# Spreading the matmul blocks of a feed-forward layer over PSUM banks

## The chip, the cores and the metric

The kernel runs on one core of one Trainium2 chip. A core has a matrix engine (TensorE, "PE" in the profile, with its weight loads listed as "PEld"), a vector engine (DVE), a scalar engine (ACT), a general engine (POOL) and a queue that issues DMAs (SP). The metric is the device time of one launch in microseconds.

Matmuls write into PSUM. The kernel uses it in tiles of 128 partitions by 512 float32 columns; one such tile is one bank, and there are eight. A matmul here is 128 by 128 weights against 256 moving columns, so its output fills half a bank.

## The reference

The reference is a two-layer encoder trunk on 256 tokens of width 1024. Each layer is a feed-forward half-step, a token mixer (retention, stick-breaking attention, a state-space mixer, and an output projection), and a second feed-forward half-step. All of them are normalised and modulated by a vector `c`. What the change touches is the feed-forward:

```
def swiglu(u, wg, wu, wd):
    return (jax.nn.silu(u @ wg) * (u @ wu)) @ wd

h = h + 0.5 * (1.0 + mod[:, :, 2]) * swiglu(u, ffn1_wg[l], ffn1_wu[l], ffn1_wd[l])
```

The inner width is 2816, which is eleven groups of 256. There are four feed-forward half-steps in all, two in each layer.

## The kernel before

Everything is kept transposed: partitions are features, columns are the 256 tokens. To keep float32 accuracy, each operand is split into a rounded part and a remainder (`hi` and `lo` of a weight, `uh` and `ul` of an activation), and each product is three matmuls onto the same output (`mm3`, L208): hi by uh, hi by ul, lo by uh. These three are the "block of three matmuls" of the change.

**Weights.** 184 units of weights of 1 MB each come from HBM by DMA in a fixed order, into tiles called `raw`, mixed with 80 units `raw_a` of the modulation matrices. `step` (L271) takes the next one. For half a weight unit, ACT makes `hi` (L322) and DVE makes `lo` (L323); for a modulation unit, DVE reduces it against the condition (L282). `half(n, f)` (L317) first emits the splits up to seven halves ahead (`AHEAD = 7`) of the half that is wanted. There are eight buffers each for `hi` and `lo`.

**Feed-forward** (`ffn`, L583). For each group `j` of 256 inner columns there are a gate weight `g`, an up weight `u` and a down weight `d`. `proj` (L567) accumulates gate over eight feature blocks `k`: for each `k`, one block of three into columns 0 to 255 of the bank `pg`, and one into columns 256 to 511, 48 matmuls in all. ACT then applies silu to the whole bank `pg` into an SBUF tile `sg` (L627, through L203). `proj` does the same for up in another bank, `pu`. DVE multiplies `sg` by `pu` (L630), and ACT and DVE split the product into the tile `g`. Where `j` is 1, gate and up are interleaved by `k` (`proj2`) before silu. The first two weight units of a half-step (in the first half-step, the first six) are done earlier, into banks `ld`, while the normalisation is still under way.

**Down.** `out_unit` (L517) takes one group: for each half `f` of it and each of eight output blocks `d`, one block of three into an accumulator `dn`. Four banks hold the eight accumulators, two to a bank, side by side (L519). It is called for earlier groups, so that the product `g` has time to be made. The last `out_unit` goes by output block, and DVE adds each finished block to the residual `h` (L539) while the later blocks are computed. The mixer's output projection uses `out_unit` too, with accumulators `wo`.

**Mixer.** Its input projections `pj` also put both blocks of a `k` into one bank. The two value projections (`pv`) have a bank for each of two token halves, and there the activations are the stationary operand and the weights move. `conv` reads a bank `pj` by halves: ACT makes the first term of each half (L715), DVE adds the others (L717). At the start of three of the half-steps `ends` fills the SBUF tile `sg` by halves in the same way (ACT through L203, DVE at L601).

**Banks.** Four banks are a ring (`bank`, L213) from which `pg` and `pu` come in turn, so that a bank comes round every second group; four are the accumulators. [...]

**Order.** Each engine runs its own instructions in the order in which the program emits them (a manual schedule). The framework puts the semaphore waits between engines in by itself, from which tiles the instructions read and write.

Of the kernel before, what the change touches and what calls it, by code (L numbers as in the profile page):

```python
# [10 lines left out]
ALU = mybir.AluOpType  # L11
PSUM = bass.MemoryType.PSUM

P = 128
# [68 lines left out]
def downs(j, g0):  # L83
    done = 0
    for i in range(g0, j + 1):
        lo = done
        done = i if i - lo <= 2 else lo + 2
    return range(lo, done)
# [74 lines left out]
class Trunk:  # L163
# [352 lines left out]

    def out_unit(self, accs, n, mov, first, last, gate):  # L517
        nc = self.nc
        dst = lambda d: accs[d // 2][:, (d % 2) * 256:(d % 2) * 256 + 256]  # L519

        def block(w, d, f):
            st = first and f == 0 and d % 2 == 0
            self.mm3(dst(d), [w[0][:, d * P:(d + 1) * P], w[1][:, d * P:(d + 1) * P]], mov[f], st)

        if not last:
            for f in range(2):
                w = self.half(n, f)
                for d in range(8):
                    block(w, d, f)
                    if d % 2:  # L530
                        self.tick()
            return
        ws = [self.half(n, 0, 7), self.half(n, 1, 6)]
        for b in range(4):
            for d in (2 * b, 2 * b + 1):
                for f in range(2):
                    block(ws[f], d, f)
            for d in (2 * b, 2 * b + 1):
                nc.vector.scalar_tensor_tensor(out=self.h[:, d], in0=dst(d), scalar=gate[:, d:d + 1], in1=self.h[:, d],  # L539
                                               op0=ALU.mult, op1=ALU.add)  # L540
            if self.hg is None and b == 2:
                nc.scalar.preload_act_table_set(SET_SQRT)
            self.norm_a(b)
            if b == 2 or self.hg and b:
                self.norm_b(b - 1)
        if self.hg:
            self.norm_b(3)
# [10 lines left out]
    def proj_k(self, bank, w, k, flip, banks):  # L558
        w = [t[:, k % 4] for t in w]
        for f in range(2):  # L560
            if flip:
                self.mm3(banks[f], w, [t[:, f * P:(f + 1) * P] for t in self.u(k)], k == 0, True)
            else:
                cs = slice(f * P, (f + 1) * P)
                self.mm3(bank[:, f * 256:(f + 1) * 256], [t[:, cs] for t in w], self.u(k), k == 0 and f == 0)
# [17 lines left out]
    def ffn(self, w0, gate_col, prep, start=None):  # L583
        nc = self.nc
        self.open_acc(False)
        n = w0 + 2
        pend = []

        def gated(sg):
            g = self.tk4("g", FR)  # L590
            gh, gl = (g[:, 2 * i:2 * i + 2] for i in range(2))
            flat = lambda t: t.rearrange("p a b -> p (a b)")
            self.split(flat(gh), flat(gl), sg)
            pend.append([(gh[:, f], gl[:, f]) for f in range(2)])

        def ends(f, t, b):
            v = sg[:, (f % 2) * 256:(f % 2) * 256 + 256]
            if f < 2:
                self.silu(out=v, in_=t, bias=b)
            else:  # L600
                nc.vector.scalar_tensor_tensor(out=v, in0=t, scalar=b, in1=v, op0=ALU.add, op1=ALU.mult)  # L601

        g0 = 1
        if start:
            g0 = GS
            banks = start()
            n = w0 + 2 * GS
            self.need(n, 0, 2)
            for j in range(GS):
                sg = self.tk2("sg")  # L610
                self.silu(out=sg, in_=banks[2 * j])
                nc.vector.tensor_tensor(out=sg, in0=sg, in1=banks[2 * j + 1], op=ALU.mult)
                gated(sg)
        else:
            sg = self.tk2("sg")
            self.lead(w0, ends)
            gated(sg)
        accs = None
        for j in range(g0, NJ):
            pg, pu = self.bank("pg"), self.bank("pu")  # L620
            pair = j == 1
            if pair:
                self.proj2(n, (pg, False, None), (pu, False, None))
            else:
                self.proj(pg, n)
            sg = self.tk2("sg")
            self.silu(out=sg, in_=pg)  # L627
            if not pair:
                self.proj(pu, n + 1)
            nc.vector.tensor_tensor(out=sg, in0=sg, in1=pu, op=ALU.mult)  # L630
            gated(sg)
            if j == g0:
                accs = [self.acc("dn") for _ in range(4)]
            n += 2
            for i in downs(j, g0):
                self.out_unit(accs, n, pend.pop(0), i == 0, False, None)
                n += 1
            if start and j == 7:
                nc.sync.dma_start(out=self.consts, in_=self.io["consts"])
                nc.sync.dma_start(out=self.wdt, in_=self.io["wdt"])  # L640
        gate = self.gate(gate_col, True)
        prep()
        self.out_unit(accs, n, pend.pop(0), False, True, gate)
        self.close_acc()
# [469 lines left out]
```

## Time and profile before

| | |
|---|---|
| three runs | 1124.79, 1131.02, 1131.15 us; median 1131.02 |
| the profiled execution | 1130.79 us, its span 1129.0 us |
| PE busy | 1094.3 us, 97% of the span, 9316 matmuls |
| DVE busy | 892.1 us, 79% |
| ACT busy | 617.4 us, 55% |
| DMA | 282.63 MB, 250 GB/s on the mean |
| mean granted TensorE clock | 0.998 |

The profile is one execution, and 1.8 us of its time lie outside the span. A row of a group view gives the source line, the engine, the output and inputs by tile name, the shapes, the count, the busy time and the mean duration of one, and then the idle time of the engine just before these instructions with what ended it. A row of the timeline gives start, length, and in brackets how long the engine had been idle and what released it. Consecutive instructions of a kind are merged there, with their count. A row of the chain of work that ended last gives start, length, engine, tile and count. A matmul's own duration overlaps the next matmul's, so the pace of PE is read from starts, or from the length of a stretch over its count.

The half-steps lie, by matmuls of gate, up and down, at 63 to 210 us (the first), 400 to 569 us, 582 to 757 us and 948 to 1116 us; the two mixers fill most of what is between.

### The profile page before, as it was taken

The page shows a single profiled execution, that of the slowest core. Times are in us where ns is not written, and L with a number is a line of the kernel's source. Part 1 is how long each engine was busy: PE and PEld are TensorE (multiplying, and loading weights), DVE is VectorE, ACT ScalarE, POOL GpSimd, SP SyncE. Part 2 cuts the span into 40 slices and gives each one's busy share as a digit, 9 for nine tenths or more (in the row PEclk, how much of TensorE's full clock was granted, in tenths as well). Part 3 has the DMA queues.
Part 4 walks back from the last instruction along what each step waited for, and adds up shares of the span by engine and source line. Part 5 has one row for each costly group of instructions (what it writes and reads, how often), then busy time and mean ns, then how long its engine had stood idle before and what let it go on. Part 6 is the DMA issues. An engine that isn't in the chain of part 4 may idle for free.

```text
span 1129.0 us, 22045 instructions
## 1 busy us (share of the span) xinstructions
PE 1094.3 (97%) x9316; PEld 1083.1 (96%) x9316; DVE 892.1 (79%) x1300; ACT 617.4 (55%) x870; POOL 0.2 (0%) x4
## 2 busy tenths in 40 slices
PE   1999999999999999999999999999999999999996
PEld 0999999999999999999999999999999999999996
DVE  6989896888778788899688888667886878987644
ACT  3463535586874464445466444457687546554442
POOL 0000000000000000000000000000000000000000
PEclk9999999999999999999999999999999999999999
DMA  9979998467454449999627888653745552898611
GB/s 374 352 262 375 364 372 332 148 222 273 177 187 150 187 145 375 355 369 365 236 97 298 337 328 320 250 185 125 285 179 196 187 187 75 337 342 325 234 69 38
DMA packets 39555, 282.63 MB, mean 250 GB/s; under 512 B 4384, under 2 KB 4640, under 8 KB 5408
## 3 DMA queue, kind: packets, MB, share of 16 engines
q1 hardware_dynamic: 39456, 281.22, 66.1%
q8 instruction: 73, 1.20, 0.4%
q14 instruction: 26, 0.21, 0.1%
HBM read 280.15 MB, written 1.05 MB: 249 GB/s over the span
## 4 chain that ended last, share of the span: by engine, by line
PE 96%; DVE 2%; ACT 1%; DMA 1%; issue 0%; SPq 0%; ACTq 0%; DVEq 0%
PE dn L206 21%; PE pg L206 18%; PE pu L206 18%; PE pj L206 14%; PE ld L206 8%; PE wo L206 6%; PE pv L206 4%; DVE raw_a L282 1%; PE seg L206 1%; PE nps L206 1%; PE tail L206 1%; PE sz L206 1%; DMA h<-in_x 1%; PE rn L206 1%; PE yb L206 1%; PE rs L206 0%
## 5 line engine op out<-in xcount | busy, mean ns | idle before, releaser
L323 DVE TENSOR_TENSOR lo<-raw_w,hi 128x1024 fp32r<-128x1024 f32 x368 | 440.9, 1222 | 126.6 <-ACT hi L322 126.0
L322 ACT ACTIVATE hi<-raw_w 128x1024 fp32r<-128x1024 f32 x368 | 379.5, 1054 | 239.8 <-DMA raw_w<-in_w 122.5
L206 PE MATMUL dn<-g,hi 128*128 128x256 f32 x1408 | 243.6, 277 | 0.0
L206 PEld LDWEIGHTS dn<-g,hi 128*128 128x128 f32 x1408 | 212.9, 188 | 0.0
L282 DVE CUSTOM_DVE_ANT_0 raw_a<-raw_a,cond,params 128x1024 f32<-128x1024 f32 x160 | 198.9, 1280 | 0.0
L206 PE MATMUL dn<-g,lo 128*128 128x256 f32 x704 | 195.2, 277 | 0.0
L206 PE MATMUL pg<-ul,hi 128*128 128x256 f32 x608 | 168.6, 277 | 0.0
L206 PE MATMUL pg<-uh,hi 128*128 128x256 f32 x608 | 168.6, 277 | 0.0
L206 PE MATMUL pg<-uh,lo 128*128 128x256 f32 x608 | 168.5, 277 | 0.0
L206 PE MATMUL pu<-uh,hi 128*128 128x256 f32 x608 | 168.5, 277 | 0.0
L206 PE MATMUL pu<-ul,hi 128*128 128x256 f32 x608 | 168.5, 277 | 0.0
L206 PE MATMUL pu<-uh,lo 128*128 128x256 f32 x608 | 168.5, 277 | 0.0
L206 PEld LDWEIGHTS dn<-g,lo 128*128 128x128 f32 x704 | 132.9, 189 | 0.0
L206 PE MATMUL pj<-uh,hi 128*128 128x256 f32 x448 | 126.4, 282 | 0.0
L206 PE MATMUL pj<-ul,hi 128*128 128x256 f32 x448 | 124.5, 278 | 0.0
L206 PE MATMUL pj<-uh,lo 128*128 128x256 f32 x448 | 124.5, 278 | 0.0
L206 PEld LDWEIGHTS pu<-uh,lo 128*128 128x128 f32 x608 | 114.8, 189 | 0.0
L206 PEld LDWEIGHTS pg<-uh,lo 128*128 128x128 f32 x608 | 114.7, 189 | 0.0
L206 PEld LDWEIGHTS pg<-uh,hi 128*128 128x128 f32 x608 | 114.1, 188 | 0.0
L206 PEld LDWEIGHTS pg<-ul,hi 128*128 128x128 f32 x608 | 114.1, 188 | 0.0
L206 PEld LDWEIGHTS pu<-uh,hi 128*128 128x128 f32 x608 | 114.1, 188 | 0.0
L206 PEld LDWEIGHTS pu<-ul,hi 128*128 128x128 f32 x608 | 114.1, 188 | 0.0
(189 smaller groups left out, 1788.7 us busy)
## 6 DMA issues: line engine op xcount, KB each, us to landing
raw_w<-in_w SPq DMA_DIRECT2D x184, 1024.0 KB, 5.5
raw_a<-in_ada SPq DMA_DIRECT2D x80, 1024.0 KB, 6.4
consts<-in_consts SPq DMA_DIRECT2D x1, 1216.0 KB, 9.6
h<-in_x SPq DMA_DIRECT2D x1, 1024.0 KB, 6.7
out<-fin SPq DMA_DIRECT2D x4, 256.0 KB, 2.3
cond<-in_c SPq DMA_DIRECT2D x1, 512.0 KB, 4.5
mats<-in_mats SPq DMA_DIRECT2D x1, 256.0 KB, 6.9
params<-in_params SPq DMA_DIRECT2D x1, 176.0 KB, 4.7
```

Source lines behind the costliest of these rows:

```text
L206: self.nc.tensor.matmul(out, lhsT=lhsT, rhs=rhs, start=start, stop=True, skip_group_check=True)
L282: nc.vector.tensor_tensor_reduce(out=raw[:, f * 1024:(f + 1) * 1024], in0=raw[:, f * 1024:(f + 1) * 1024], in1=self.cond, scale=1.0, scala ...
L322: self.nc.scalar.activation(out=hi, in_=src, func=AF.Copy)
L323: self.nc.vector.tensor_tensor(out=lo, in0=src, in1=hi.bitcast(F32), op=ALU.subtract)
```

## The change

Gate and up of a group no longer have a bank each. The group takes two banks from the ring (now tagged by the name `pgu`); gate uses columns 0 to 255 of both, up uses columns 256 to 511 of both. So the two blocks of three of one `k` go to different banks. silu and the multiplication become two instructions of 256 columns each, one per bank. In `out_unit`, accumulator `d` goes to bank `d % 4`, half `d // 4`, where it was bank `d // 2`, half `d % 2`, so consecutive blocks go round the four banks. The `start` flags follow: gate sets them at `k` 0 on both banks, up on none, and down on blocks 0 to 3. `proj` and `proj_k` get `flip=None` for the new layout, with the last argument used as the flag for `start`.

```
     def out_unit(self, accs, n, mov, first, last, gate):
-        dst = lambda d: accs[d // 2][:, (d % 2) * 256:(d % 2) * 256 + 256]
+        dst = lambda d: accs[d % 4][:, (d // 4) * 256:(d // 4) * 256 + 256]
 
         def block(w, d, f):
-            st = first and f == 0 and d % 2 == 0
+            st = first and f == 0 and d < 4
...
             if flip:
                 self.mm3(banks[f], w, [t[:, f * P:(f + 1) * P] for t in self.u(k)], k == 0, True)
+            elif flip is None:
+                cs = slice(f * P, (f + 1) * P)
+                self.mm3(bank[f], [t[:, cs] for t in w], self.u(k), k == 0 and banks)
...
         for j in range(g0, NJ):
-            pg, pu = self.bank("pg"), self.bank("pu")
+            two = [self.bank("pgu") for _ in range(2)]
+            pg, pu = ([t[:, o:o + 256] for t in two] for o in (0, 256))
             pair = j == 1
             if pair:
-                self.proj2(n, (pg, False, None), (pu, False, None))
+                self.proj2(n, (pg, None, True), (pu, None, False))
             else:
-                self.proj(pg, n)
+                self.proj(pg, n, None, True)
             sg = self.tk2("sg")
-            self.silu(out=sg, in_=pg)
+            for f in range(2):
+                self.silu(out=sg[:, f * 256:(f + 1) * 256], in_=pg[f])
             if not pair:
-                self.proj(pu, n + 1)
-            nc.vector.tensor_tensor(out=sg, in0=sg, in1=pu, op=ALU.mult)
+                self.proj(pu, n + 1, None, False)
+            for f in range(2):
+                v = sg[:, f * 256:(f + 1) * 256]
+                nc.vector.tensor_tensor(out=v, in0=v, in1=pu[f], op=ALU.mult)
             gated(sg)
```

## The prediction

> **What bounds the kernel now.** I read the page's busy times and the shares of the chain first.
>
> ```profile
> span 1129.0 us, 22045 instructions
> PE 1094.3 (97%) x9316; PEld 1083.1 (96%) x9316; DVE 892.1 (79%) x1300; ACT 617.4 (55%) x870; POOL 0.2 (0%) x4
> PE 96%; DVE 2%; ACT 1%; DMA 1%; issue 0%; SPq 0%; ACTq 0%; DVEq 0%
> ```
>
> PE is the chain. A gain must make PE's matmuls closer together; any wait put in front of a matmul is lost time. So the next view is the chain in order of time, for the pace.
>
> ```profile
> 73.93 10.88 PE dn L206 x96
> ...
> 310.39 4.09 PE pv L206 x36
> 314.48 2.83 PE pj L206 x24
> ...
> 599.05 5.65 PE pg L206 x48
> 604.71 5.65 PE pu L206 x48
> ...
> 915.58 19.08 PE wo L206 x162
> ```
>
> The same 256-column matmul runs at two paces: 10.88/96 = 113.3 ns, and 5.65/48 = 117.7 ns. The third half-step (582 to 757 us) runs slow from its first `dn` to its last, the other three fast. Some 1,390 matmuls at 4.4 ns more are 6.2 us, and the three runs before lie 6.2 to 6.4 us apart in just this way (1124.79 against 1131.02 and 1131.15): the pace of a half-step looks drawn by chance. The rows `pv` and `pj` at 310 us are the best argument for the change: `pv` sends alternate blocks to alternate banks and runs at 113.6 ns, and `pj`, with both blocks in one bank, follows at once at 117.9 ns (`pv` also has its operands swapped, so banks need not be the reason).
>
> **The pace: what banks could bring.** Against it stands `dn` in the slow half-step:
>
> ```profile
> 594.18 0.28 PE L206 MATMUL dn<-g,lo 128*128 128x256 f32 x1
> 594.30 0.40 PE L206 MATMUL dn<-g,hi 128*128 128x256 f32 x2
> 594.53 0.28 PE L206 MATMUL dn<-g,lo 128*128 128x256 f32 x1
> 594.65 0.40 PE L206 MATMUL dn<-g,hi 128*128 128x256 f32 x2
> 594.88 0.28 PE L206 MATMUL dn<-g,lo 128*128 128x256 f32 x1
> ```
>
> Every second of these blocks already changes bank. The last matmuls of three blocks start at 594.18, 594.53 and 594.88, every 0.35 us, whether the bank changes or not. So a change of bank saves nothing by itself; at most full alternation keeps PE out of the slow pace. If it does everywhere, the third half-step gains 6.2 us and the slow stretches of `wo` (162 in 19.08 us is 117.8 ns) about 1 us in each mixer: -8. If it does not, each new wait of PE (below) draws the pace anew, and the worst end is the three fast half-steps all slow, +18. The nearest row by banks (`pv`) says -8; the nearest by operands (`dn`, slow) says no effect, and then half slow is about +4. I take -2.
>
> **The change, the part that costs: PE now waits for silu.** Before, silu reads bank `pg` while PE writes bank `pu`. After, PE's first `pu` block goes to the other half of the bank that silu is reading. Does the program make PE wait? Four rows show how accesses to two halves of one tile are ordered:
>
> ```profile
> 242.94 1.00 ACT L715 ACTIVATE conv<-pj,params 128x256 f32<-128x256 f32 x2
> 243.98 1.26 DVE L717 SCALAR_TENSOR_TENSOR conv<-pj,params,conv 128x255 f32<-128x255 f32 x3 [0.78 <-ACT conv L715]
> ...
> 407.02 0.91 ACT L203 ACTIVATE sg<-lt,lbias 128x256 f32<-128x256 f32 x2
> 407.57 0.88 DVE L601 SCALAR_TENSOR_TENSOR sg<-lt,lbias,sg 128x256 f32<-128x256 f32 x2 [1.34 <-ACT sg L203]
> ...
> L715 ACT ACTIVATE conv<-pj,params x16: 549/556/569, 242.9 to 839.0; 128x256 f32<-128x256 f32 x16
> ```
>
> In the lower pair the tile is in SBUF. DVE needs only the first half, and starts at 407.57, before ACT's second half ends at 407.93. In the upper pair both engines read one PSUM bank. DVE's first instruction needs only columns 0 to 255, which ACT's first instruction ended at 242.94 + 0.55 = 243.49; it starts at 243.98, just after the second, on the other half, ended at 243.94. So PSUM is ordered by bank, even between two readers. I take it that a write behind a read is ordered alike, though no instruction of this kernel shows that pair.
>
> [...]
>
> **Price of one wait, ACT free.** Rows of a group where ACT was waiting:
>
> ```profile
> 1034.79 0.28 PE L206 MATMUL pg<-uh,lo 128*128 128x256 f32 x1
> 1034.90 0.28 PE L206 MATMUL pu<-uh,hi 128*128 128x256 f32 x1
> 1035.10 0.60 ACT L203 ACTIVATE sg<-pg 128x512 f32<-128x512 f32 x1 [1.72 <-PE pg L206]
> ...
> L918 ACT ACTIVATE rv<-pv 128x256 f32<-128x256 f32 x8 | 2.9, 385 | 3.8 <-PE pv L206 3.8
> ...
> 27.10 0.58 PE L206 MATMUL ld<-uh,hi 128*128 128x256 f32 x1 [10.35 <-ACT hi L322]
> ```
>
> silu starts 0.31 us after the start of gate's last matmul. After the change the first bank's last matmul is three earlier, at -0.34, so the first silu starts at -0.03. A 256-column ACT read of PSUM takes 0.385, so it ends at 0.36; PE follows ACT by about 0.05 (ACT's first `hi` before 27.10 ended near 27.05), so `pu` starts at 0.41 where it started at 0.11: 0.30 us. The second silu ends 0.35 to 0.45 later (the pair at 242.94 takes 1.00 where one takes 0.55), and its bank is wanted 0.34 later: 0 to 0.1 more, which I count as none. There are 35 such groups (8 in the first half-step, 9 in each other; the interleaved group has no wait): 35 x 0.30 = 10.5 us. Queued behind the waiting matmul is all of PE: the rest of up, down and the next gate.
>
> **Price when ACT is late.** ACT works in order, and ahead of silu stand the splits of weights seven halves ahead.
>
> ```profile
>   PE pg L206: 29.1, 17
> ...
> 422.05 0.28 PE L206 MATMUL pg<-uh,lo 128*128 128x256 f32 x1
> ...
> 424.86 2.01 ACT L322 ACTIVATE hi<-raw_w 128x1024 fp32r<-128x1024 f32 x2 [4.50 <-DMA raw_w<-in_w]
> 431.87 1.06 ACT L322 ACTIVATE hi<-raw_w 128x1024 fp32r<-128x1024 f32 x1 [5.00 <-DMA raw_w<-in_w]
> 432.84 0.58 ACT L203 ACTIVATE sg<-pg 128x512 f32<-128x512 f32 x1
> ...
> 519.97 0.28 PE L206 MATMUL pg<-uh,lo 128*128 128x256 f32 x1
> 526.47 0.58 ACT L203 ACTIVATE sg<-pg 128x512 f32<-128x512 f32 x1
> ...
> 969.51 0.28 PE L206 MATMUL pg<-uh,lo 128*128 128x256 f32 x1
> 976.80 0.58 ACT L203 ACTIVATE sg<-pg 128x512 f32<-128x512 f32 x1
> ```
>
> The first row, of the waits before instructions on `sg`, says that ACT waited for gate in only 17 of 38 groups. In the others it came late, and before that cost nothing. At 422.05 gate was done; ACT stood waiting for weights from DMA, and silu came 10.79 us later. Now PE would stand there with it: 10.79 + 0.385 + 0.05 - 0.11 = 11.1 us. At 969.51 it is 7.29 + 0.33 = 7.6 us. These delays do not add up over later groups: ACT is paced by the DMA, not by PE, so once PE has lost 11.1 us the later lags of that half-step, down to 6.5 at 526.47, are covered. So a half-step pays its largest lag once, and 0.30 for every other group. The second and the fourth pay 10.8 and 7.3 beyond the 0.30. In the first the largest lag is
>
> ```profile
> 111.74 0.28 PE L206 MATMUL pg<-uh,lo 128*128 128x256 f32 x1
> 114.72 0.58 ACT L203 ACTIVATE sg<-pg 128x512 f32<-128x512 f32 x1
> ```
>
> 2.98, of which 0.6 is paid by the 0.30s before it: 2.4 (if the lags there add instead, I estimate up to 8.5). The third starts with weights in hand, and I count nothing for it. Together 20.5.
>
> **PE's clock after the two long gaps.**
>
> ```profile
> 28.60:32.60 4.00, 4.00 (x20) 4.00 (x21) 4.00 (x4) 4.00 (x5) 0.00 (x0) 1.00 1.01 422
> 33.00:62.00 29.00, 29.00 (x259) 29.00 (x258) 26.64 (x39) 12.55 (x17) 0.00 (x0) 1.00 0.86 327
> ```
>
> After the idle 10.35 us before 27.10, PE did 20 matmuls in 4.0 us, 200 ns each, and then 112 ns; some 22 matmuls at 100 ns more are about 2.1 us. (The granted clock, third column from the end, reads 1.00 in both rows; the pace tells the difference.) Two gaps, 11.1 and 7.6 us, the second shorter than the one seen: 4.2, between 0 and 4.2. [...]
>
> **The tail.** In the last `out_unit`, block 4 now shares block 0's bank, and PE must wait for DVE's read of it.
>
> ```profile
> 206.81 0.48 DVE L539 SCALAR_TENSOR_TENSOR h<-dn,gate,h 128x256 f32<-128x256 f32 x1
> ...
> 199.05 10.88 PE dn L206 x96
> ```
>
> The unit ends at 209.93, so its last matmul starts at 209.65, and block 4, 23 matmuls (2.61 us) before, at 207.04. The read ends at 207.29, and 0.05 later PE may go: 0.3 us. Over six tails I estimate 0.7. The extra silu and multiplication cost ACT and DVE about 0.14 us a group, beside PE's 16 us for it: nothing.
>
> **Sum.** 10.5 + 20.5 + 4.2 + 0.7 - 2 = 33.9; 1130.8 + 33.9 = 1164.7. The profiled execution is 0.2 us from the median, so **1165 us**.
>
> **Rivals.**
> 1. *No wait* (on the other side): write and read of two halves are not ordered. Then PE never stops and only the pace moves: 1130.8 - 8 = 1123, or 1131 without effect. It decides if the wait on the bank holds for two readers only. Against it: the 243.98 row. Chance 0.10, both together.
> 2. *Short waits only*: ACT's lags vanish, because weights arrive earlier once PE is slower. 1130.8 + 10.5 + 0.7 - 2 = 1140. Against it: at 422 us the DMA, not PE, is what ACT waits for. 0.08.
> 3. *Lags add up*: ACT is held by PE after all, and each late silu is paid in full. In the second half-step seven groups lie between the lags of 10.79 and 6.50 that are shown, these two included; seven times their mean of 8.6 is 60, 50 more than I count: 1165 + 50 = 1215. Against it: only DMA is named as ACT's releaser there. 0.06.
>
> The forecast has 0.76. Its own spread: pace -8 to +18, clock 0 to 4.2, first half-step 2.4 to 8.5; low 1165 - 6 - 4 = 1155, high 1165 + 20 + 6 = 1191 if all fall together, which I cut to 1183. Downwards I reach to 1145, towards rival 2. A difference under 1% (11 us) could hardly be told from none here: slower by over that 0.85 (forecast, rival 3, a part of rival 2), within 0.11, faster 0.04.
>
> **What would show it.** In the chain, gaps of PE before the first `pgu` matmul of up, ended by ACT's silu: about 0.3 us in most groups, near 11 us in the second half-step's third group and 7 in the fourth's. Silu there in two parts of some 0.39 us. The matmuls of gate, up and down at 113 ns in all four half-steps would prove the bank effect. If PE shows no gap ended by ACT, the wait was my error.

## The result: 3.5% slower, and the profile after

Four runs after took 1165.73, 1166.19, 1166.66 and 1168.95 us (median 1166.43), four runs before 1124.49, 1124.79, 1131.02 and 1131.15. The ratio of after to before is 1.0346, interval (95%) 1.0301 to 1.0391. Here and below, a ratio leaves out executions that took over 1.5% longer than the fastest of their kernel. The profiled execution after took 1166.66 us, 35.9 us more than the profiled one before.

The page of the kernel after: the span, the busy times, the granted clock in 40 slices, the shares of the chain, and one row of the groups (busy time and mean ns of one; idle time before them and what ended it).

```profile
span 1164.9 us, 22112 instructions
PE 1104.0 (95%) x9316; PEld 1085.4 (93%) x9316; DVE 896.9 (77%) x1338; ACT 626.2 (54%) x908; POOL 0.2 (0%) x4
...
PEclk9999999999999998999999999999999999899998
...
PE 84%; DVE 7%; ACT 4%; DMA 3%; issue 1%; SPq 0%; ACTq 0%; DVEq 0%
...
L203 ACT ACTIVATE sg<-pgu 128x256 f32<-128x256 f32 x76 | 26.8, 381 | 37.4 <-PE pgu L206 37.3
```

PE has the same 9316 matmuls, but it is 84% of the chain where it was 96%: the chain now runs through ACT and, behind it, through DVE and DMA. silu is 76 instructions of 0.381 us. ACT is busy 8.8 us more than before and DVE 4.8 us, 0.23 and 0.13 us for each of the 38 groups, where the prediction has about 0.14. What PE waits for stands in the view of the waits (waiting engine and tile, releaser, total us, count, longest):

```profile
PEld pgu L206 <- ACT sg L203: 33.4, 35, 10.8
...
PEld dn L206 <- DVE h L539: 0.9, 3, 0.3
```

35 waits for silu, the count of the prediction, and the longest 10.8 us. One of the ordinary ones, in PE's timeline (start, length) and then ACT's:

```profile
1119.22 0.28 PE L206 MATMUL pgu<-uh,lo 128*128 128x256 f32 x1
1119.63 0.39 PE L206 MATMUL pgu<-uh,hi 128*128 128x256 f32 x1
1119.85 0.28 PE L206 MATMUL pgu<-ul,hi 128*128 128x256 f32 x1
1119.97 0.28 PE L206 MATMUL pgu<-uh,lo 128*128 128x256 f32 x1
```

```profile
1119.19 0.72 ACT L203 ACTIVATE sg<-pgu 128x256 f32<-128x256 f32 x2 [1.38 <-PE pgu L206]
```

The first row is gate's last matmul, the second up's first. Their starts are 0.41 us apart where PE's pace is 0.113. The first silu starts at 1119.19, before gate's last matmul, as the prediction had it (-0.03). The gap behind the restart (up's first matmul after the wait), 0.22, is also too long: a second loss of 0.11 us, which the prediction did not have. From the third gap on PE is back at 0.11 to 0.12.

The longest wait, in the second half-step, PE's timeline and ACT's:

```profile
428.68 0.28 PE L206 MATMUL pgu<-uh,lo 128*128 128x256 f32 x1
439.60 0.58 PE L206 MATMUL pgu<-uh,hi 128*128 128x256 f32 x1 [10.64 <-ACT sg L203]
439.98 0.42 PE L206 MATMUL pgu<-ul,hi 128*128 128x256 f32 x1
440.19 0.41 PE L206 MATMUL pgu<-uh,lo 128*128 128x256 f32 x1
```

```profile
431.50 2.00 ACT L322 ACTIVATE hi<-raw_w 128x1024 fp32r<-128x1024 f32 x2 [4.56 <-DMA raw_w<-in_w]
...
438.22 1.06 ACT L322 ACTIVATE hi<-raw_w 128x1024 fp32r<-128x1024 f32 x1 [4.72 <-DMA raw_w<-in_w]
439.18 0.64 ACT L203 ACTIVATE sg<-pgu 128x256 f32<-128x256 f32 x2
```

Gate is done at 428.96, and ACT stands twice, 4.56 and 4.72 us, waiting for weights that are wanted only later; silu is queued behind them and starts at 439.18. The gap is 10.92 us. Behind it PE is slow, in the view by windows (length; PE busy and count; granted clock, DMA share, GB/s):

```profile
440.00:444.80 4.80, 4.80 (x24) 0.50 1.01 420
445.60:458.00 12.40, 12.40 (x112) 1.00 0.75 289
1000.70:1004.70 4.00, 4.00 (x20) 0.50 0.93 385
```

After the gaps of 10.9 and 7.7 us the matmuls come every 200 to 213 ns for some 4.5 us, and here the granted clock goes with it: 0.50. A gap of 2.35 us in the first half-step is not followed by this: behind it, from the third matmul on, the starts are 0.11 to 0.12 us apart, at a granted clock of 1.00.

The chain in the third half-step and at the last `wo` blocks:

```profile
646.01 5.73 PE pgu L206 x48
651.74 5.44 PE dn L206 x48
657.18 5.11 PE pgu L206 x45
662.32 0.39 ACT sg L203
...
938.56 19.22 PE wo L206 x162
```

`dn` is at 5.44/48 = 113.3 ns where it was 117.7, and each group passes once through ACT. So this half-step was fast this time; the other three were fast before and stayed so. `wo` now goes round four banks too, and stays slow: 162 matmuls in 19.22 us, where they took 19.08.

**The balance**, from the starts of PE's matmuls against the profiled execution before, in us:

| | after | forecast |
|---|---|---|
| 35 waits: 0.296 + 0.109 (restart) each | 14.2 | 10.5 |
| late silu beyond that (half-steps 1 to 4: 3.2, 10.5, 0.9, 7.3) | 21.9 | 20.5 |
| slow clock (25 and 21 matmuls, some 0.1 us more each) | 4.7 | 4.2 |
| tails (three half-steps, `dn` waits for `h`) | 1.1 | 0.7 |
| pace (third half-step slow before, fast after) | -6.2 | -2 |
| sum | 35.7 | 33.9 |
| measured between the two profiled executions | 35.9 | |

### The profile page after: what moved, and what is told of

It is laid out like the page before. It is cut to its first block, busy times and chain, and to the rows that moved or that the text cites. A ratio compares the mean times of both kernels' runs of the same rounds, so it can differ in the third digit from the quotient of the medians.

```text
span 1164.9 us, 22112 instructions
## 1 busy us (share of the span) xinstructions
PE 1104.0 (95%) x9316; PEld 1085.4 (93%) x9316; DVE 896.9 (77%) x1338; ACT 626.2 (54%) x908; POOL 0.2 (0%) x4
## 4 chain that ended last, share of the span: by engine, by line
PE 84%; DVE 7%; ACT 4%; DMA 3%; issue 1%; SPq 0%; ACTq 0%; DVEq 0%
PE pgu L206 31%; PE dn L206 18%; PE pj L206 13%; PE ld L206 7%; PE wo L206 6%; PE pv L206 4%; DMA raw_w<-in_w 2%; DVE lo L323 2%; ACT hi L322 2%; DVE raw_a L282 2%; ACT sg L203 1%; DVE nt L462 1%; PE seg L206 1%; DVE ul L468 1%; PE nps L206 1%
## 5 line engine op out<-in xcount | busy, mean ns | idle before, releaser
L206 PE MATMUL pgu<-uh,hi 128*128 128x256 f32 x1216 | 342.1, 281 | 26.5 <-ACT sg L203 22.5
L206 PE MATMUL pgu<-ul,hi 128*128 128x256 f32 x1216 | 338.0, 278 | 0.0
L206 PE MATMUL pgu<-uh,lo 128*128 128x256 f32 x1216 | 337.8, 278 | 0.0
L206 PEld LDWEIGHTS pgu<-uh,hi 128*128 128x128 f32 x1216 | 230.5, 190 | 33.4 <-ACT sg L203 33.4
L206 PEld LDWEIGHTS pgu<-ul,hi 128*128 128x128 f32 x1216 | 230.7, 190 | 0.0
L206 PEld LDWEIGHTS pgu<-uh,lo 128*128 128x128 f32 x1216 | 230.4, 189 | 0.0
L206 PEld LDWEIGHTS pj<-uh,hi 128*128 128x128 f32 x448 | 84.6, 189 | 0.7 <-issue 0.7
L206 PEld LDWEIGHTS pj<-ul,hi 128*128 128x128 f32 x448 | 84.2, 188 | 0.0
L206 PEld LDWEIGHTS pj<-uh,lo 128*128 128x128 f32 x448 | 84.2, 188 | 0.0
L323 DVE TENSOR_TENSOR g<-sg,g 128x512 fp32r<-128x512 f32 x44 | 30.5, 693 | 30.7 <-ACT g L322 30.7
```

Of the source, the lines that this page charges most:

```text
L206: self.nc.tensor.matmul(out, lhsT=lhsT, rhs=rhs, start=start, stop=True, skip_group_check=True)
L323: self.nc.vector.tensor_tensor(out=lo, in0=src, in1=hi.bitcast(F32), op=ALU.subtract)
```

## The experiments

The theory: the time is PE's wait for silu on a shared bank, plus the late silu of two or three groups; the alternation of banks gains little or nothing. Its rivals: the alternation itself, or the round of four in `down`, costs or gains; or the late silus are not what makes the long gaps.

Runs of the kernel before stood beside each experiment, with a median of 1137.39 us for the first four, 1131.11 for the next four and 1138.05 for the last; the ratios go by these runs. The first expectations were written from 1124 to 1131, so a time can lie above its expectation while the ratio is 1.

### Alternation without sharing

```
-            two = [self.bank("pgu") for _ in range(2)]
-            pg, pu = ([t[:, o:o + 256] for t in two] for o in (0, 256))
+            pg = [self.bank("pg")[:, 0:256] for _ in range(2)]
+            pu = [self.bank("pu")[:, 0:256] for _ in range(2)]
...
-                self.proj(pu, n + 1, None, False)
+                self.proj(pu, n + 1, None, True)
```

This is the changed kernel with gate and up in two banks each, all four of the ring, so every block still alternates.

> Gate keeps its two banks by halves of 256 columns, but up goes to the two other banks of the ring, so that blocks still alternate banks and silu never reads a bank that up writes. Theory (PE waits for silu because both are in one bank): the 35 gaps of PE before up go away, and the time returns to that of before, 1124 to 1133 us; where silu or the multiplication is 11 us late in the second half-step, the next group may still wait 1 to 2 us for its banks. Rival (the split of silu and multiplication in two, or the alternation itself, costs): it stays near 1166. On the pace: if alternating banks keep PE at 113 ns, all executions lie together near 1124 to 1126; if the pace of a half-step is drawn by chance, they fall into values some 6 us apart as those of before do (1124.5 and 1131).

Measured: median 1137.6 us in 12 runs (1127.08 to 1140.77); ratio to before 0.9978, interval 0.9945 to 1.0011. The waits of the kernel with four banks:

```profile
PEld pu L206 <- DVE lt L502: 2.0, 3, 0.7
...
PEld dn L206 <- DVE h L539: 0.8, 3, 0.3
```

No wait for silu is left, and with it goes the whole loss. (The row of 2.0 us is up waiting for its banks at the start of three half-steps.) The same execution also answers the other half of the question. Its chain in the first half-step, in the third, and in the second mixer's output projection:

```profile
111.36 5.44 PE pu L206 x48
...
641.22 5.65 PE pu L206 x48
646.88 5.65 PE dn L206 x48
652.53 5.65 PE pg L206 x48
...
918.38 11.66 PE wo L206 x99
```

In all rows the blocks change bank. The lower ones run at the slow pace of 117.7 to 117.8 ns; in the first two half-steps of the same execution the same code ran at 113.3. So alternation does not hold the fast pace. The 23 runs of the kernel before beside it say the same from the other side: they lie near 1124.4 (one), 1131 (two), 1136.6 to 1138.5 (18) and 1144 us (two), in steps of about 6.3 us, which is what one slow half-step costs.

### Each half of the change alone

Gate and up as changed, `down` as before:

```
-        dst = lambda d: accs[d % 4][:, (d // 4) * 256:(d // 4) * 256 + 256]
+        dst = lambda d: accs[d // 2][:, (d % 2) * 256:(d % 2) * 256 + 256]
...
-            st = first and f == 0 and d < 4
+            st = first and f == 0 and d % 2 == 0
```

> Gate and up as changed, down and the output projection with the old layout of two neighbouring blocks in a bank. Theory: gate and up carry all but the tails, so 1164 to 1166 us, about 1 to 2 us below the full change. Rival (the new order of the down accumulators costs something too): below 1160.

Measured: 1183.71 us (1181.88 to 1187.2, 4 runs), ratio 1.0404, interval 1.0364 to 1.0444. This was missed by 17 to 20 us. The waits are the same as in the full change:

```profile
PEld pgu L206 <- ACT sg L203: 32.3, 35, 9.7
```

Their gaps add up to 39.5 us against 41.9. What differs is the pace of nearly everything else; the chain of this kernel in the third half-step:

```profile
648.05 5.31 PE pgu L206 x45
653.38 0.39 ACT sg L203
653.82 5.92 PE pgu L206 x48
659.74 5.65 PE dn L206 x48
```

`dn` is at 117.7 ns, and so are some 63% of the matmuls of the second half-step and 81 to 92% of those of the others. That is the miss: the execution is 53.1 us over the one before, 39.5 of it gaps and 13.6 left for the pace, where some 82% of the 25 us that four slow half-steps cost, less the 6.2 that the execution before had, would give 14.

The other half, `down` and `wo` round four banks with gate and up as before:

```
-        dst = lambda d: accs[d // 2][:, (d % 2) * 256:(d % 2) * 256 + 256]
+        dst = lambda d: accs[d % 4][:, (d // 4) * 256:(d // 4) * 256 + 256]
...
-            st = first and f == 0 and d % 2 == 0
+            st = first and f == 0 and d < 4
```

> Only the down and output-projection accumulators go round four banks; gate and up as before. Theory: no wait in the groups; in the last unit of a half-step PE waits for the read of block 0 by 0.3 us in three places, so 0.5 to 1.5 us more than before, 1125 to 1133 us, with the same two values some 6 us apart. Rival (going round banks keeps the fast pace): all executions near 1124 to 1126, and the output projection near 113 ns a matmul where it was 117.3.

Measured: 1137.29 us (1125.7 to 1139.31, 12 runs), ratio 0.9983, interval 0.9947 to 1.0018: no difference. Its chain in the first half-step and in the third:

```profile
113.28 5.65 PE pu L206 x48
...
643.64 5.44 PE pg L206 x48
649.08 5.44 PE pu L206 x48
654.52 5.44 PE dn L206 x48
```

Gate and up keep a bank each in this kernel, and are slow in one half-step and fast in another. So the round of four makes no difference that these runs could tell (about half a per cent) where no waits are. The 0.5 to 1.5 us that the expectation gives to the last units are too small for that.

### The wait without the alternation

```
-            pg, pu = self.bank("pg"), self.bank("pu")
             pair = j == 1
+            pg = self.bank("pg")
+            pu = self.bank("pu") if pair else pg
```

This is the kernel before, with up written into gate's own bank: nothing alternates, and PE must wait for the whole silu of 512 columns.

> The layout of before (both blocks of a step in one bank, one silu of 512 columns), but up is written into the same bank that gate had, in all groups but the interleaved one. Nothing alternates; only the wait is there. Theory: PE waits for the whole silu, 0.31 + 0.59 + 0.05 - 0.11 = 0.84 us and some 0.11 of restart, 35 times: 33 us; the late silus of 11 and 8 us and the slow clock after them, some 25 us: about 1183 us from a fast-paced 1125. If blocks that do not change bank fall into the slow pace after each wait, up to 20 us more. Rival (alternation, not the wait, is what costs): 1124 to 1133.

Measured: 1193.64 us (1190.38 to 1196.34, 4 runs), ratio 1.0486, interval 1.0445 to 1.0527. The waits:

```profile
PEld pg L206 <- ACT sg L203: 47.8, 35, 10.1
```

Again 35. The ordinary gap is 0.962 to 0.968 us, 0.85 more than a pace of 0.113, and the next one is again 0.11 too long. All gaps, with the slow clock behind the two longest, add up to 54.6 us, of 59.6 between this profiled execution (1190.38) and the one before. The rest fits the pace: about half of the stretches between waits are slow, some 12 of the 25 us that four slow half-steps cost, where the execution before had 6.2. The time is 10 us over the 1183 expected, inside the "up to 20 us more" for a slow pace. Nearly everywhere fast and slow stretches take turns, as `dn` between the waits of the second half-step shows:

```profile
469.41 5.65 PE dn L206 x48
...
487.13 5.44 PE dn L206 x48
...
504.62 5.65 PE dn L206 x48
...
522.34 5.44 PE dn L206 x48
```

That a bank shared by gate and up costs by itself is shown.

### The late silus

The splits that stand ahead of silu in ACT's queue are those of later weights. In the changed kernel, four halves ahead instead of seven:

```
-    AHEAD = 7
+    AHEAD = 4
```

> The changed kernel, with the splits of weights emitted four halves ahead instead of seven. Theory (silu is late because splits of weights that have not arrived stand before it on ACT): the long gaps of PE shrink by about three halves of transfer, some 8 us: from 10.9 to 1 to 4 us in the second half-step, from 7.7 to under 1 in the fourth, with the slow clock after them gone too. So 17 to 24 us less than 1166, 1142 to 1150, if the mixers don't suffer from the shorter lookahead (the next kernel shows that). Rival (PE's gaps are from something else than ACT's queue): about 1166.

Measured: 1150.62 us (1149.58 to 1164.83, 4 runs), ratio 1.021, interval 1.0141 to 1.028. The waits of this kernel, and ACT's timeline at the place of the longest wait:

```profile
PEld pgu L206 <- ACT sg L203: 11.8, 35, 0.4
...
PEld dn L206 <- DVE h L539: 4.7, 3, 1.6
```

```profile
429.87 2.01 ACT L322 ACTIVATE hi<-raw_w 128x1024 fp32r<-128x1024 f32 x2 [1.26 <-DMA raw_w<-in_w]
432.92 0.67 ACT L203 ACTIVATE sg<-pgu 128x256 f32<-128x256 f32 x2 [1.03 <-PE pgu L206]
```

silu is now released by PE, not by weights, and no wait for silu is over 0.4 us: the gaps of 10.9 and 7.7 us are 0.47. All 35 waits are still there. The three waits of `dn` for `h` have grown, from 0.9 to 4.7 us together, with gaps of 1.56 to 1.67 us. That DVE's read of `dn` now stands behind splits, as silu did on ACT before, is the author's reading; no view here shows it. The sum of the gaps falls from 41.9 to 19.2 us. The profiled execution, with 1164.83 us the slowest of the four, is mostly at the slow pace, some 74% of the matmuls of the half-steps, with the same banks as the full change, whose matmuls held 113.3 ns; the other three took 1149.6 to 1151.5. The kernel before with the same edit:

> The kernel before with four halves ahead: the price of the shorter lookahead alone, in gaps of PE before matmuls whose weights are not split. Theory: before, late silus cost nothing, so nothing is gained here; the same values as before (1124, 1131, 1137, 1144), or some us more where weights come late. If this gains as much as the kernel with the change does, the lookahead and not the late silu is the reason.

Measured: 1134.44 us (1128.24 to 1146.35, 10 runs), ratio 1.0021, interval 0.9981 to 1.0062. A shorter lead gained nothing here (1.0021), where PE does not wait for silu; the fastest runs are 1128.2 with it and 1123.8 without. So what it gains in the changed kernel is the late silus. This kernel also has the one long stretch of `wo` that ran fast: 162 matmuls in 18.37 us in the first mixer, with two blocks side by side in each bank.

### The order of the two silus

```
-            for f in range(2):
+            for f in (1, 0):
                 self.silu(out=sg[:, f * 256:(f + 1) * 256], in_=pg[f])
```

Up's first block goes to the first bank, and here silu reads the second bank first, so PE waits for both.

> The changed kernel, with silu of the second bank emitted before silu of the first. Theory: the first silu now waits for gate's very last matmul, and PE needs the second to end: 0.31 + 0.38 + 0.35 + 0.05 - 0.11 = 0.98 us of wait where it was 0.30, so 35 x 0.68 = 24 us more: 1190. The pace of each stretch after a wait is drawn anew, so if the 113 ns of the changed kernel came from the moment of restart and not from its banks, slow stretches (118 ns) appear again, up to 20 us more. If alternating banks keep the pace, all stretches stay at 113.

Measured: 1199.54 us (two runs, 1198.70 and 1200.38), ratio 1.0614, interval 1.0532 to 1.0696.

```profile
PEld pgu L206 <- ACT sg L203: 52.5, 35, 10.6
```

The ordinary gap is 1.023 to 1.029 us instead of 0.41: some 0.615 more, where 0.68 was expected. The five late silus are not lengthened by as much, one of them not at all, so all gaps add up to 60.7 us against 41.9: 18.8 of the 32 us between the two profiled executions (1198.70 and 1166.66). The rest fits the pace, since 40 to 78% of the matmuls of the half-steps are slow here, 49% over all, and of the 25 us that four slow half-steps cost this is 12.

### One wait in each half-step

If a restart after a wait sets the pace, one early restart in a half-step might do. Gate and up as before, `down` round four banks, and the changed layout in one early group of each half-step only, with a short lead up to there:

```
+            once = j == (GS if start else 2)
+            self.AHEAD = 4 if j < GS + 1 else 7
+            if once:
+                pg, pu = ([t[:, o:o + 256] for t in two] for o in (0, 256))
+            else:
+                pg, pu = ([t[:, o:o + 256] for o in (0, 256)] for t in two)
```

> The layout of before for gate and up, down going round four banks, and the changed layout in one early group of each half-step only, with four halves ahead up to there. So PE waits once in each half-step, by 0.4 us where silu is in time, and the pace is drawn there once. Theory: 4 waits, 1.6 us, and up to 5 us where silu is still late; if the restart after this wait leads into the fast pace as it did 35 times in the changed kernel, all executions lie at 1127 to 1132, below the middle of before (1137 on the chip of the last runs); if it does not, values some 6 us apart as before, plus 2 to 6 us.

Measured: 1128.45 us in the median of 12 runs, seven of them at 1127.4 to 1128.45 and four at 1132.8 to 1136.0 (the twelfth took 2247.53 us; it has no profile, and is not explained). The ratio is 1.0003, interval 0.9967 to 1.0039. The waits of this kernel and its chain in the third half-step:

```profile
PEld pgu L206 <- ACT sg L203: 1.8, 4, 0.7
```

```profile
644.95 5.44 PE dn L206 x48
650.39 10.88 PE pgu L206 x96
```

Four waits of 1.8 us in all, and all four half-steps fast, where the profiled execution before had one slow and that of the four banks two. But it takes back about 3.6 us: its lowest time, 1127.44, is above the lowest before beside it (1123.8). It is no faster version. The same with `down` as before:

> The last kernel (one wait of PE in each half-step) with the old layout of down, which takes away the waits in the last units: 1 to 1.5 us less, 1126 to 1127 where all half-steps are fast. Theory: the wait's restart draws the pace by its moment, so whether it is fast here is open: if the moments are as in the last kernel, most executions lie at 1126 to 1127; if the restarts go as in the kernel with the changed gate and up alone (slow after 410 ns), most half-steps are slow and it comes to 1140 to 1150. If alternating banks mattered, this kernel, which alternates in four groups only, would spread as before does.

Measured: 1149.1 us (1145.0 to 1152.22, 6 runs), ratio 1.0118, interval 1.0068 to 1.0168. Its chain in the third half-step:

```profile
640.82 11.31 PE pgu L206 x96
652.13 5.65 PE dn L206 x48
```

The one restart is there and three of four half-steps are slow. So a restart does not by itself bring the fast pace. In the two profiled executions it did not even change the pace: the matmuls right ahead of the restart run as those behind it in all eight half-steps, fast in five, slow in three. What set the pace there lies ahead of the wait.

## Why the prediction was right, and where its sizes were off

- **The place of the wait: right.** In this program a write to one half of a bank waited for a read of the other half, 35 times and 33.4 us in all; this pair was not in the trace before, and the prediction inferred it from two readers. (A bank is always one whole PSUM tile in this kernel, so "by bank" and "by PSUM tile" are not told apart.) The four banks take the wait away, the single bank makes it without alternation (47.8 us), the order of the silus lengthens it (52.5 us). Rival 1 (no wait) is out.
- **The price of one wait: the wait right, the restart missing.** 0.296 us measured, 0.30 forecast. The step "`pu` starts at 0.41 where it started at 0.11" stopped there; the next matmul loses another 0.109. Over 35 waits the term is 14.2 instead of 10.5.
- **The late silus: right.** 10.5 and 7.3 us beyond the ordinary wait, against 10.8 and 7.3. The second and fourth half-steps pay their largest lag once, and no later group there shows a long gap: rival 3 (the lags add up, 1215) is out. Rival 2 (weights come earlier to a slower PE, 1140) is out as well, since ACT still waits 4.56 and 4.72 us for weights at that place; only the shorter lead takes the lag away. In the first half-step there were two gaps, 2.35 and 1.63, and 3.2 us instead of 2.4: there two lags were paid, not the largest alone. The third, which was counted at nothing, paid 0.9.
- **The clock: right.** Both gaps were followed by half speed, 4.7 against 4.2 us, and this time the granted clock shows it (0.50), where it read 1.00 in the row that the prediction went by. That the shorter gap would pay as well was the author's estimate from that one row, behind 10.35 us of idle time; no row of the kernel before shows it. In the kernel after, 21 matmuls were slow behind a gap of 7.7 us and none behind 2.35 us.
- **The tails: the count wrong, the sum about right.** Three waits of `dn` for `h`, not six tails, at 0.31 to 0.41 us each including the restart: 1.1 instead of 0.7.
- **The pace: the step that failed, though the sum hides it.** "The pace of a half-step looks drawn by chance" stands, as to its size; the argument from `pv` and `pj` that alternation could hold PE in the fast pace does not. With four banks every block alternates and two half-steps are slow; `wo` goes round four banks and is as slow as before, and ran fast once with the old layout. The term was -6.2 instead of -2, and cancelled most of what the other four terms cost over the forecast: -4.2 against +6.0. That the forecast is so near is luck: it lies 1.4 us from the median, with errors of three to four times that inside it.
- The test named for the bank effect ("at 113 ns in all four half-steps would prove" it) was too weak. All four were at 113, and the four banks and the short lead show the same alternation at 117.7. One profiled execution can't prove a bank effect where executions of one kernel differ in just this way.

**What stays open** is the pace after a restart. The starts of the matmuls around each wait of up show this much:

- Where the stretch ahead of the wait was fast, the second gap (the one behind the restart) goes with the next stretch in every kernel, the half clock aside: behind 220 to 223 ns it is fast, behind 225 or 226 ns slow. The first gap does not tell: it is 409 or 410 ns in the full change, whose 33 restarts at full clock all led into fast stretches, and 410 ns in seven restarts with `down` as before, which all led into slow ones. The second gaps differ by about the 4.4 ns between the two paces, so the longer one may be the first of the slow gaps rather than their cause.
- Where the stretch ahead was slow, the kernels differ: with `down` as before 19 of 22 ordinary restarts stayed slow, and in the single bank all 14 became fast.

Two pairs point to `down` round four banks: waits everywhere, 1166.4 with it and 1183.7 without; one wait, 1128.5 and 1149.1. That is 17 to 21 us, across runs in which the fastest runs before were alike (1123.8 to 1125.1); by the ratios, whose medians before moved with the pace (1127.9, 1137.4, 1131.1, 1138.1), it is 0.6 and 1.2%, and the intervals of the first pair overlap. But by itself it gains nothing (0.9983), and one execution with the short lead was mostly slow in spite of it. Why the two together are mostly fast was not settled.

## What to carry to other kernels

In this program a PSUM bank acted as one lock: where two consecutive phases shared its halves, the engine that reads the first phase held up the writer of the second, 35 times and 33.4 us in all, and no wait for silu was left where each had banks of its own. So in a program like this one list the reader of every bank before changing who shares it. The base price (0.4 us a group, 14.2 us in all) was small beside what came where the reader was late for a reason of its own (21.9 us, and 4.7 us of slow clock): look in the reader's queue for work that is issued ahead and waits for DMA, because here the writer stood there with it, 10.9 and 7.7 us, where a shorter lead left 0.47. And look at several runs for steps of one size before putting a few microseconds down to an edit.

## What the runs showed of the hardware

- **Two lasting paces.** The same stream of 128 by 128 weights and 256 columns runs at 113.3 or at 117.7 ns a matmul, mostly for a half-step at a time, with every layout of banks tried. In the profile before, the granted clock is 1.00 in a fast stretch (73.9 to 84.8 us) and in a slow one (604.7 to 610.3 us). The runs of one kernel therefore fall on steps of about 6.3 us (before: 1124.4, 1131, 1137 to 1138, 1144). The profiled executions with no wait for silu fit: one slow half-step at 1130.79, two at 1136.93 and 1140.49, three at 1146.35 us, which is 5.6 to 6.7 us for each over the fastest run of the kernel in question.
- **A restart costs twice.** Behind each wait of up of 0.3 to 2.5 us the second gap between matmuls was 0.22 us instead of 0.113 (in the kernel after, gaps of 0.41 and 0.22 us at 1119.22, and of 2.35 and 0.22 us at 67.72).
- **Half clock after an idle time**, as a granted clock of 0.50 in the windows of the kernel after (440.0 to 444.8 and 1000.7 to 1004.7 us): 25 matmuls after a gap of 10.9 us and 21 after 7.7 us, 2.6 and 2.1 us lost; none after 2.35 us. The same pace of 213 ns followed all six gaps of 7.0 to 10.7 us in the three other kernels with late silus and seven halves ahead.
